# Eight low-part subtractions of the weight split, in four panels of the sparse attention, moved from VectorE to GpSimd

## The chip, the cores and the metric

The kernel runs on one core of a Trainium2 chip. The metric is the device time of one execution in microseconds. The core's engines are named as the profile names them: PE (TensorE, matmuls), PEld (its weight loads), DVE (VectorE), ACT (ScalarE), POOL (GpSimd) and SP (SyncE, which here issues most DMAs).

## The reference, cut to what matters

Two layers follow each other, each a token mixer, a layer norm, a squared-ReLU MLP and a layer norm. Layer 0 mixes tokens by a sparse attention: an indexer scores all earlier keys of a query, the best 128 are kept, and softmax attention runs over them. 512 tokens, model width 1024, all in 32-bit floats.

```python
def dsa_mixer(x, cos, sin, w_in, w_o):
    top_k = min(IDX_TOPK_MAX, L // 4)                 # 128
    proj = x @ w_in                                   # 512 x 1024 @ 1024 x 2120
    q, k, v, iq, ik, iw = jnp.split(proj, A_SPLITS, axis=-1)
    q, k, iq, ik = (partial_rotary(t, cos, sin) for t in (q, k, iq, ik))
...
    s = einsum('bqhd,bsd->bqhs', iq_b, ik) * IDX_DIM ** -0.5
    score = einsum('bqh,bqhs->bqs', iw_b, relu(s))    # causal keys only
    _, sel = lax.top_k(score, top_k)
    logits = einsum('bqgrd,bqkgd->bqgrk', q_b, k_sel) * A_HEAD_DIM ** -0.5
    p = softmax(logits)
    o = einsum('bqgrk,bqkgd->bqgrd', p, v_sel)
...
    return out @ w_o

for i in range(DEPTH):
    mix = dsa_mixer(h, ...) if i % 2 == 0 else gla_mixer(h, ...)
    h = layer_norm(DN_ALPHA * h + mix, ...)
    h = layer_norm(DN_ALPHA * h + squared_relu_mlp(h, ...), ...)
```

## The kernel before, in words

Every product of activations and weights is made of three matmuls on numbers rounded to the fast 32-bit format: high part by high part, high by low, low by high (`mm3`, lines 183 to 188). A weight matrix comes in panels, most of them 512 columns wide. A panel is loaded in four units of 256 rows by 512 columns (128 partitions by 1024 elements). For each unit SP issues one DMA into a `raw` tile (4 buffers), ACT rounds it into `w_hi` (line 130, 6 buffers), and DVE subtracts, `w_lo = raw - w_hi` (line 131, 6 buffers). `split` does the last two, `_load` loops over the two halves `ci` of a panel's rows and over `u`, the two units of each half. Below, "unit (p,n)" is the n-th of the four units of panel p, counted from 0: n is 2 ci + u, so u = 1 means n = 1 or 3.

`next_panel` loads one panel ahead: when the matmuls of panel p begin in the program, the instructions that load panel p+1 have just been written. The panels of the attention are 0 and 1 (indexer projections), 2 (keys and values), 3 and 4 (the two halves of the queries), 5 and 6 (output projection). The framework's scheduler then sets the order of the instructions on each engine, by its own estimates of when operands are ready; the engines work through these orders strictly one after the other and wait for each other by semaphores. The printed code is therefore not the order on an engine.

What stands around the loads in the attention, all of it on DVE as well:
- for each token tile of a projection `rotated` (lines 539 to 553) makes `rot_c`, `rot_s` and `nat`, and `stack_q` or `stack_k` form a high and a low part (`hl` in line 560, `dup` in line 578), which PE transposes (lines 567, 587) one tile later;
- `index_scores` (lines 609 to 622): PE makes `qk` for each of eight indexer heads (lines 613, 614; two buffers), ACT applies relu into `r` (line 616; two buffers), and DVE adds it to the scores `sc` (lines 618, 620);
- `top_k` (lines 655 to 665): for each of the query blocks 1 to 3, sixteen rounds of MAX8 (line 660) and MATCH_REPLACE8 (line 661) on the scores; the block widths are 256, 384 and 512 keys. A result of MAX8 is named `m_` and a number, in rising order; `sc_216`, `sc_217` and `sc_218` are the scores of blocks 1, 2 and 3;
- `logits` (lines 670 to 692): PE makes `qk`, DVE adds the mask and takes the maximum (line 685), ACT the exponential.

GpSimd is used elsewhere: in the MLP (`_load_forms`, lines 152 to 160, four subtractions of 128x1024 for every `down` panel but the last; `combine`), in the second layer's mixer, and for DMAs of layer norm parameters (lines 312, 313).

Of the kernel before, what the change touches and what calls it, by code (L numbers as in the profile page):

```python
# [14 lines left out]
F32 = mybir.dt.float32  # L15
# [8 lines left out]
P = 128  # L24
# [35 lines left out]
WARM_UP = (4, 6)  # L60
STACKED = 2
LAG = 3

_CF = {}

# [29 lines left out]
class Trunk:  # L95
# [26 lines left out]
            n += m  # L122
        return raw[:, :, :n]

    def split(self, src):

        n = src.shape[2]
        hi = self.w_p.tile([P, 2, 512], F32R, name="w_hi")[:, :, :n]
        lo = self.w_p.tile([P, 2, 512], F32R, name="w_lo")[:, :, :n]
        self.nc.scalar.copy(hi, src)  # L130
        self.nc.vector.tensor_sub(lo, src, hi.bitcast(F32))  # L131
        return hi, lo

    def _load(self, i):
        panel = self.panels[i]
        if isinstance(panel, tuple):
            return self._load_forms(*panel)
        units = {}
        for ci, (w, r0, nk, cols) in enumerate(panel):
            for u in range(nk // 2):  # L140
                hi, lo = self.split(self.fetch(w, r0 + 2 * u * P, cols))
                for j in range(2):
                    units[(ci, 2 * u + j)] = (hi[:, j, :], lo[:, j, :])
        return units
# [448 lines left out]
    def attention(self, x, xs):  # L593

        nc, tc = self.nc, self.tc
        with tc.tile_pool(name="att", bufs=1) as ap:
# [143 lines left out]
            def values_t(i, kb):  # L740

                b, g = steps[i]
                if kb == 0:
                    live["o"] = self.mm.tile([P, 512], F32, name="ps")
                ps = live["o"]
                ph, pl = (a.rearrange("p j q -> p (j q)") for a in live.pop((i, kb)))
                vs = live["vs"][:, kb * A_KV + g]
                vs = vs.rearrange("p two d -> p (two d)")
                nc.tensor.matmul(ps, vs, ph, start=kb == 0, stop=False)
                nc.tensor.matmul(ps, vs, pl, start=False, stop=kb == b)  # L750
                for f in live.pop("back", []):
                    f()
                if kb == b:
                    oT = ptp.tile([P, 4, P], F32, name="pT")
                    nc.scalar.copy(oT, ps.rearrange("p (j q) -> p j q", j=4))

                    def back():
                        po = self.po.tile([P, 512], F32, name="po").rearrange("p (j d) -> p j d", d=P)
                        for j in range(4):
                            nc.tensor.transpose(po[:, j, :], oT[:, j, :], self.ident)  # L760
                        on, rc = normalizer(b, g, live[i][2])
                        nc.scalar.copy(on, po[:, :, 64:128])
                        nc.vector.tensor_add(on, on, po[:, :, 0:64])
                        nc.vector.tensor_tensor(on, on, rc, op=OP.mult)
                        if g == A_KV - 1:
                            self.to_xt(live["on"], b)

                    live["back"] = [back]

            def blocks():  # L770
# [4 lines left out]
                for i, (b, g) in enumerate(steps):  # L775
                    if (b, g) == (STACKED, 0):
                        split_v()
                    for x in range(4):
                        if i + 1 < len(steps):
                            logits(i + 1, x)  # L780
                        if x <= b:
                            turn(i, x)
                            if b >= STACKED:
                                turned.append((i, x))
                        if len(turned) > LAG:
                            values_t(*turned.pop(0))
# [365 lines left out]
```

## Time and profile before

| | us |
|---|---|
| time, median of 3 executions (lowest to highest) | 1173.49 (1171.34 to 1174.58) |
| the profiled execution's own time | 1171.8 |
| its span, from the first to the last instruction | 1170.0 |
| PE busy in the span | 1147.4 |
| DVE busy | 901.1 |
| ACT busy | 559.3 |
| POOL busy | 213.8 |

The profile is of one execution. The busy times are of the whole span; an engine that is full in one stage and half idle in another shows a middling share. Matmuls are pipelined, so a PE that is shown busy may still have waited: its waits stand in the view of waits. The granted TensorE clock is shown as a share of full speed; over the span its mean is 0.996.

### The profile page before, as it was taken

Reading aid. Unit: us, or ns where it says so; the run is one execution under the profiler, and the core shown is the slowest. Engines: PE = TensorE matmul, PEld = TensorE weight load, DVE = VectorE, ACT = ScalarE, POOL = GpSimd, SP = SyncE. Lnnn points to the kernel's source line nnn. Section 1 sums busy time; section 2 is a strip of 40 time slices with the busy share of each in tenths; the row PEclk is TensorE's granted clock in tenths of the full one; section 3 lists DMA queues with packets and bytes.
Section 4 is the critical chain, followed back from the end, with each engine's and each line's share of the span. In section 5 each row is a group of like instructions: output and inputs, shape, how many; then the busy total and the mean of one; then the engine's idle time right before and its main releaser. Section 6 shows DMA issues by size and latency. Waiting matters only on the chain. (4 is left out here: it accounts for less than half of the span.)

```text
span 1170.0 us, 15763 instructions
## 1 busy us (share of the span) xinstructions
PE 1147.4 (98%) x5847; PEld 963.3 (82%) x5847; DVE 901.1 (77%) x1659; ACT 559.3 (48%) x953; POOL 213.8 (18%) x148
## 2 busy tenths in 40 slices
PE   8999999999999999999899999999999999999997
PEld 6877888888888888888788998778988888888875
DVE  6799997687876786687875477885787866886787
ACT  6665786543444353345356444443354533444342
POOL 0000000002223203222302254110032032223221
PEclk9999999999999999999999999999999999999999
DMA  5422130421431441243341231224214422431421
GB/s 199 142 73 73 36 109 1 144 73 37 144 99 46 143 141 64 84 144 94 91 133 49 61 104 41 73 75 142 73 54 127 140 64 85 144 103 44 142 72 73
DMA packets 57477, 109.36 MB, mean 93 GB/s; under 512 B 4708, under 2 KB 10088, under 8 KB 57400
## 3 DMA queue, kind: packets, MB, share of 16 engines
q1 hardware_dynamic: 56008, 103.44, 27.8%
q0 software_dynamic: 1392, 4.92, 1.4%
q8 instruction: 46, 0.75, 0.3%
q14 instruction: 31, 0.25, 0.1%
HBM read 106.24 MB, written 2.10 MB: 93 GB/s over the span
## 5 line engine op out<-in xcount | busy, mean ns | idle before, releaser
L131 DVE TENSOR_TENSOR w_lo<-raw,w_hi 128x1024 fp32r<-128x1024 f32 (+4 forms) x220 | 289.1, 1333 | 30.1 <-ACT w_hi L130 27.7
L130 ACT CAST w_hi<-raw 128x1024 fp32r<-128x1024 f32 (+4 forms) x220 | 223.6, 1024 | 117.7 <-PE ps L188 46.0
L186 PE MATMUL ps<-XT,w_hi 128*128 128x512 f32 (+1 forms) x640 | 236.0, 369 | 0.0
L187 PE MATMUL ps<-XT,w_hi 128*128 128x512 f32 (+1 forms) x640 | 235.5, 368 | 0.0
L188 PE MATMUL ps<-XT,w_lo 128*128 128x512 f32 (+1 forms) x640 | 235.5, 368 | 0.0
L186 PE MATMUL ps<-w_hi,XT 128*128 128x512 f32 (+5 forms) x440 | 164.3, 374 | 2.0 <-ACT XT L230 1.6
L187 PE MATMUL ps<-w_lo,XT 128*128 128x512 f32 (+5 forms) x440 | 161.7, 368 | 0.4 <-DVE w_lo L131 0.4
L188 PE MATMUL ps<-w_hi,XT 128*128 128x512 f32 (+5 forms) x440 | 161.2, 367 | 0.3 <-DVE XT L231 0.2
L186 PEld LDWEIGHTS ps<-XT,w_hi 128*128 128x128 f32 x640 | 120.7, 189 | 20.3 <-issue 0.2
L187 PEld LDWEIGHTS ps<-XT,w_hi 128*128 128x128 f32 x640 | 120.7, 189 | 20.2 <-issue 0.4
L188 PEld LDWEIGHTS ps<-XT,w_lo 128*128 128x128 f32 x640 | 120.6, 189 | 20.1 <-issue 0.2
L152 POOL TENSOR_TENSOR raw<-raw 128x1024 f32<-128x1024 f32 x14 | 34.2, 2441 | 385.3 <-DVE w_lo L131 385.3
L186 PE MATMUL ps<-w_hi,form 128*128 128x512 f32 x260 | 102.2, 393 | 0.7 <-DVE big L405 0.7
L187 PE MATMUL ps<-w_lo,form 128*128 128x512 f32 x260 | 101.4, 390 | 0.0
L188 PE MATMUL ps<-w_hi,form 128*128 128x512 f32 x260 | 101.4, 390 | 0.0
L186 PEld LDWEIGHTS ps<-w_hi,XT 128*128 128x128 f32 x440 | 83.3, 189 | 13.5 <-ACT XT L230 2.3
L188 PEld LDWEIGHTS ps<-w_hi,XT 128*128 128x128 f32 x440 | 83.4, 190 | 11.5 <-DVE XT L231 0.4
L187 PEld LDWEIGHTS ps<-w_lo,XT 128*128 128x128 f32 x440 | 83.4, 190 | 10.6 <-DVE w_lo L131 0.6
L131 DVE TENSOR_TENSOR w_lo<-t,w_hi 128x1024 fp32r<-128x1024 f32 x14 | 30.2, 2160 | 72.8 <-ACT w_hi L130 72.8
L357 DVE TENSOR_TENSOR h<-h 128x512 f32<-128x512 f32 (+1 forms) x72 | 43.7, 624 | 45.3 <-ACT h L356 45.3
L356 ACT ACTIVATE h<-ps 128x512 f32<-128x512 f32 (+1 forms) x72 | 38.6, 545 | 63.1 <-PE ps L188 56.1
L130 ACT CAST w_hi<-t 128x1024 fp32r<-128x1024 f32 x14 | 14.7, 1051 | 105.3 <-POOL t L154 105.3
(243 smaller groups left out, 2006.0 us busy)
## 6 DMA issues: line engine op xcount, KB each, us to landing
raw<-in_mlp_w_up_dram SPq DMA_DIRECT2D x64, 512.0 KB, 4.2
raw<-in_mlp_w_down_dram SPq DMA_DIRECT2D x64, 512.0 KB, 4.3
raw<-in_b_w_in_dram SPq DMA_DIRECT2D x16, 512.0 KB, 4.3
raw<-in_a_w_in_dram SPq DMA_DIRECT2D x12, 512.0 KB, 4.2
big<-in_x_dram SPq DMA_DIRECT2D x8, 512.0 KB, 4.1
raw<-in_a_w_o_dram SPq DMA_DIRECT2D x8, 512.0 KB, 4.6
raw<-in_b_w_o_dram SPq DMA_DIRECT2D x8, 512.0 KB, 4.9
raw<-in_b_w_in_dram SPq DMA_DIRECT2D x8, 346.0 KB, 3.7
```

What stands on the lines that cost most here:

```text
L130: self.nc.scalar.copy(hi, src)
L131: self.nc.vector.tensor_sub(lo, src, hi.bitcast(F32))
L152: sub(t1, b12, b11)
L186: mmul(out, lhs[0], rhs[0], start=first, stop=False, skip_group_check=more)
L187: mmul(out, lhs[0], rhs[1], start=False, stop=False, skip_group_check=more)
L188: mmul(out, lhs[1], rhs[0], start=False, stop=last, skip_group_check=more)
L356: nc.scalar.activation(h, ps[:, :step], AF.Relu)
L357: nc.vector.tensor_mul(h, h, h)
```

## The change

Units with u = 1 of the panels 2 to 5 get their low part on GpSimd; all other low parts stay on DVE. That is two units of four in four panels: eight instructions.

```diff
+POOL_PANELS = range(2, 6)
...
-    def split(self, src):
+    def split(self, src, pool=False):
...
         self.nc.scalar.copy(hi, src)
-        self.nc.vector.tensor_sub(lo, src, hi.bitcast(F32))
+        (self.nc.gpsimd if pool else self.nc.vector).tensor_sub(lo, src, hi.bitcast(F32))
...
-                hi, lo = self.split(self.fetch(w, r0 + 2 * u * P, cols))
+                hi, lo = self.split(self.fetch(w, r0 + 2 * u * P, cols), i in POOL_PANELS and u == 1)
```

The first added line moves the lines behind it by one: what is L131 before is L132 in the changed kernel. The scheduler makes new orders for all engines. Three places of them follow.

On POOL, from the start of the program, before (the DMAs are those of the layer norm parameters, the subtraction behind them the first of the MLP):

```order
L312 DMA lngb<-in_ln_mix_g_dram 128x1024
L313 DMA lngb<-in_ln_mix_b_dram 128x1024
L312 DMA lngb<-in_ln_mlp_g_dram 128x1024
L313 DMA lngb<-in_ln_mlp_b_dram 128x1024
L152 ISA
L152 TENSOR_TENSOR raw<-raw 128x1024
```

and in the changed kernel:

```order
L132 ISA
L132 TENSOR_TENSOR w_lo<-raw,w_hi 128x1024 x8
L313 DMA lngb<-in_ln_mix_g_dram 128x1024
L314 DMA lngb<-in_ln_mix_b_dram 128x1024
L313 DMA lngb<-in_ln_mlp_g_dram 128x1024
L314 DMA lngb<-in_ln_mlp_b_dram 128x1024
```

The eight subtractions stand ahead of everything that POOL did before.

On DVE, where the second half of panel 2 and the first half of panel 3 are split, with buffer numbers, before (`w_lo_486` is unit (2,2), `w_lo_492` (2,3), `w_lo_674` (3,0), `w_lo_680` (3,1)):

```order
L131 TENSOR_TENSOR w_lo_486<-raw_483,w_hi_485 128x1024
L131 TENSOR_TENSOR w_lo_492<-raw_489,w_hi_491 128x1024
L560 TENSOR_TENSOR hl_575<-nat_568,hl_575 128x5x64
L131 TENSOR_TENSOR w_lo_674<-raw_671,w_hi_673 128x1024
L550 TENSOR_TENSOR rot_c_614<-ps_578,cos_93 128x80
L551 TENSOR_TENSOR rot_s_615<-ps_578,sin_92 128x80
L131 TENSOR_TENSOR w_lo_680<-raw_677,w_hi_679 128x1024
L552 TENSOR_TENSOR nat_612<-rot_c_614,rot_s_615 128x5x16
L618 TENSOR_SCALAR sc1_216<-r_625,iw_230 128x256
```

and in the changed kernel:

```order
L132 TENSOR_TENSOR w_lo_486<-raw_483,w_hi_485 128x1024
L561 TENSOR_TENSOR hl_575<-nat_568,hl_575 128x5x64
L132 TENSOR_TENSOR w_lo_674<-raw_671,w_hi_673 128x1024
L551 TENSOR_TENSOR rot_c_614<-ps_578,cos_93 128x80
L552 TENSOR_TENSOR rot_s_615<-ps_578,sin_92 128x80
L553 TENSOR_TENSOR nat_612<-rot_c_614,rot_s_615 128x5x16
L619 TENSOR_SCALAR sc1_216<-r_625,iw_230 128x256
L561 TENSOR_TENSOR hl_619<-nat_612,hl_619 128x5x64
```

Two subtractions are gone from DVE's order; the rest stands as before. The two that are gone run on POOL while DVE is between these rows.

On DVE, where the third token tile of the second half of the queries (panel 4) gets its low part, `hl`, before:

```order
L661 MATCH_REPLACE sc_218<-m_1832,sc_218 128x512
L550 TENSOR_TENSOR rot_c<-ps,cos 128x128
L551 TENSOR_TENSOR rot_s<-ps,sin 128x128
L660 MAX m_1835<-sc_218 128x8
L552 TENSOR_TENSOR nat<-rot_c,rot_s 128x8x16
L661 MATCH_REPLACE sc_218<-m_1835,sc_218 128x512
L660 MAX m_1886<-sc_218 128x8
L131 TENSOR_TENSOR w_lo<-raw,w_hi 128x1024
L560 TENSOR_TENSOR hl<-nat,hl 128x8x64
L131 TENSOR_TENSOR w_lo<-raw,w_hi 128x1024
L661 MATCH_REPLACE sc_218<-m_1886,sc_218 128x512
```

and in the changed kernel:

```order
L661 MAX m_1892<-sc_218 128x8
L662 MATCH_REPLACE sc_218<-m_1892,sc_218 128x512
L551 TENSOR_TENSOR rot_c<-ps,cos 128x128
L552 TENSOR_TENSOR rot_s<-ps,sin 128x128
L661 MAX m_1895<-sc_218 128x8
L553 TENSOR_TENSOR nat<-rot_c,rot_s 128x8x16
L662 MATCH_REPLACE sc_218<-m_1895,sc_218 128x512
L664 TENSOR_SCALAR sc_218<-sc_218 128x512
L132 TENSOR_TENSOR w_lo<-raw,w_hi 128x1024
L561 TENSOR_TENSOR hl<-nat,hl 128x8x64
L132 TENSOR_TENSOR w_lo<-raw,w_hi 128x1024
```

All rounds of the selection for block 3 now stand ahead of this `hl` (the last is `m_1895`, and line 664 closes it), where before the rounds of `m_1886` (its MATCH_REPLACE), `m_1889`, `m_1892` and `m_1895` came behind it. On PE the same transposes stand at the same counts of projection matmuls, but for two groups that moved ahead by 5 and by 3 matmuls, and the eight heads of the first index scores, which stand closer together.

## Rows read from the trace of the kernel before

**Rows 1.** The page, part 1: busy us, share of the span and instructions of each engine.

```profile
PE 1147.4 (98%) x5847; PEld 963.3 (82%) x5847; DVE 901.1 (77%) x1659; ACT 559.3 (48%) x953; POOL 213.8 (18%) x148
```

**Rows 2.** Windows: stretch, length, busy us of PE, PEld, DVE, ACT, POOL; clock, DMA.

```profile
30.00:40.00 10.00, 10.00 (x69) 9.98 (x68) 4.08 (x11) 4.83 (x12) 0.00 (x0) 0.94 0.52 182
40.00:137.00 97.00, 95.32 (x513) 77.35 (x512) 94.33 (x272) 61.15 (x123) 0.00 (x0) 1.00 0.21 66
137.00:180.00 43.00, 42.40 (x303) 37.09 (x302) 39.63 (x123) 38.10 (x94) 0.00 (x0) 1.00 0.30 99
180.00:270.00 90.00, 89.63 (x530) 77.06 (x529) 62.67 (x143) 45.54 (x95) 2.27 (x4) 1.00 0.22 71
```

**Rows 3.** Waits of PE and PEld from 40 to 180: total us, times, longest.

```profile
PE qk L683 <- DVE mx L685: 0.8, 3, 0.4
...
PEld qk L613 <- ACT r L616: 2.7, 10, 0.5
PEld qk L683 <- DVE mx L685: 2.6, 6, 0.8
```

**Rows 4.** Waits of PE and PEld from 137 to 180.

```profile
PE tps L698 <- DVE XT L231: 0.3, 1, 0.3
...
PEld tps L698 <- DVE XT L231: 0.6, 1, 0.6
...
PEld tps L698 <- DVE pT L707: 0.3, 1, 0.3
```

**Rows 5.** DVE groups by form, 40 to 270: count, busy us, mean ns, idle before.

```profile
L131 DVE TENSOR_TENSOR w_lo<-raw,w_hi 128x1024 fp32r<-128x1024 f32 x24 | 28.8, 1218 | 1.7 <-ACT w_hi L130 1.6
...
L660 DVE MAX8 m<-sc 128x8 f32<-128x512 f32 x16 | 11.0, 685 | 0.1
L661 DVE MATCH_REPLACE8 sc<-m,sc 128x512 f32<-128x512 f32 x16 | 10.8, 676 | 0.0
...
L661 DVE MATCH_VALUE_LOAD sc<-m,sc 128x8 f32 x48 | 4.1, 85 | 0.6
...
L663 DVE TENSOR_SCALAR sc<-sc 128x512 f32<-128x512 f32 x1 | 0.4, 420 | 0.0
```

**Rows 6.** Line 131, the whole span: ns lowest/median/highest, first and last start.

```profile
L131 DVE TENSOR_TENSOR w_lo<-raw,w_hi x220: 700/1210/3477, 8.1 to 1136.1; 128x1024 fp32r<-128x1024 f32 x100, 128x692 fp32r<-128x692 f32 x4, 128x528 fp32r<-128x528 f32 x2, 128x640 fp32r<-128x640 f32 x2
...
L131 DVE TENSOR_TENSOR w_lo<-t,w_hi x14: 1208/2315/2325, 288.4 to 1107.9; 128x1024 fp32r<-128x1024 f32 x14
```

**Rows 7.** Timeline of POOL and of DVE in the first MLP: start, us, line.

```profile
276.59 2.72 POOL L152 TENSOR_TENSOR raw<-raw 128x1024 f32<-128x1024 f32 x1 [56.33 <-DVE w_lo L131]
279.39 2.74 POOL L154 TENSOR_TENSOR t<-raw 128x1024 f32<-128x1024 f32 x1
...
276.37 0.68 DVE L374 TENSOR_TENSOR big<-h 128x512 f32<-128x512 f32 x1
277.08 2.77 DVE L375 TENSOR_TENSOR big<-big,h 128x512 f32<-128x512 f32 x1
```

**Rows 8.** Timeline: POOL with DVE quiet (318.10), POOL beside a PSUM-reading DVE (559.35).

```profile
318.10 2.39 POOL L152 TENSOR_TENSOR raw<-raw 128x1024 f32<-128x1024 f32 x1 [20.52 <-DVE w_lo L131]
...
559.35 2.55 POOL L444 TENSOR_TENSOR big<-big 128x512 f32<-128x512 f32 x2
...
559.35 0.67 DVE L445 TENSOR_TENSOR big<-big,qk 128x512 f32<-128x512 f32 x1
```

**Rows 9.** Timeline of ACT and DVE at the second place of the change.

```profile
42.15 1.06 ACT L130 CAST w_hi<-raw 128x1024 fp32r<-128x1024 f32 x1
...
42.94 0.23 DVE L550 TENSOR_TENSOR rot_c<-ps,cos 128x80 f32<-128x80 f32 x1
...
44.38 0.23 DVE L552 TENSOR_TENSOR nat<-rot_c,rot_s 128x80 f32<-128x80 f32 x1
```

**Rows 10.** Timeline of DVE and PE at the third place of the change.

```profile
136.10 0.68 DVE L560 TENSOR_TENSOR hl<-nat,hl 128x512 fp32r<-128x512 f32 x1
...
137.76 0.80 PE L567 MATMUL tps<-ident_r,hl 128*128 128x128 f32 x8
```

## The prediction, made before the changed kernel ran

> **What bounds the kernel now.** First the page's busy times [rows 1]: PE is busy for 1147.4 of 1170.0 us, so nothing that frees another engine can help except where PE waits for that engine. Then the attention by windows [rows 2]. From 40 to 137 us DVE is busy for 94.33 of 97.00 us, from 137 to 180 for 39.63 of 43.00; before 40 it is less than half busy, after 180 at 70%. POOL does nothing up to 180. The eight subtractions that move lie in this stretch, the first at 30 us, the others from 40 to 137. So DVE is nearly full where the change takes work from it. The third view is what PE waits for there [rows 3]: of 140 us only 0.8 and 2.6 us are put to the maxima that DVE takes of the logits, and 2.7 us to ACT's relu in the index scores, which in its turn waits for DVE to free `r`. The reader is to see a gap between the two: DVE is full, but PE hardly waits for it, because DVE has a backlog, the rounds of the selection, that the scheduler has fitted in between what PE needs soon. The sum is therefore made along DVE, up to a place where PE takes something from it.
>
> **The change, part by part.** The place is the `hl` of the third token tile of panel 4 (third place of the change). DVE makes it at 136.10, it ends at 136.78, and PE begins its transposes at 137.76 [rows 10]: 1.0 us of slack.
>
> What leaves DVE ahead of it: seven subtractions of 1.218 us [rows 5], 8.5 us; the eighth, unit (5,3), lies behind. One of the seven, (2,1), lies at 30 us, where DVE is idle for 6 of 10 us [rows 2], and gives nothing. That leaves 6 x 1.218 = 7.3 us.
>
> What comes ahead of it: in the order on DVE all rounds for block 3 now precede it. Four MATCH_REPLACE8 of 0.676 with their value loads of 0.085, three MAX8 of 0.685 and line 664's 0.420 [rows 5]: 2.7 + 0.3 + 2.1 + 0.4 = 5.5 us. These are not new work: they stood behind it and are missing there. So DVE reaches this `hl` only 7.3 - 5.5 = 1.8 us earlier, if nothing else happens.
>
> What else happens: POOL needs 2.39 us for a subtraction of this size with DVE quiet [rows 8], and while it runs, DVE doesn't get on with some of its own. In the MLP a DVE subtraction of a size that takes 0.68 us just before, issued at 277.08, during a POOL subtraction that ends at 279.31, takes 2.77 us, and POOL's next one, issued at 279.39, then takes 2.74 [rows 7]. Over the whole span the longest `w_lo` is 3.477 us against a median of 1.210, and those that read `t`, issued when POOL is half through, take 2.315 [rows 6]. They read both operands from SBUF. An operation of the same size as the 0.68 us ones that reads one operand from PSUM takes 0.67 us beside POOL [rows 8]. So a DVE operation with two SBUF operands stands until POOL is done, and since DVE works in order, all that is behind it stands too. When both want to begin, the one that waited goes first: POOL's op at 276.59 was issued during a DVE op that ran to 277.05, and got in ahead of the one at 277.08.
>
> The price of one subtraction on POOL lies between 0 (DVE has 2.4 us of other work at hand) and 3.477 - 1.210 = 2.27 us (the next operation is of that kind); 1.1 us (2.315 - 1.210) is the middle case. For the six this is 0 to 13.6 us. I take it from the new order. (2,3) starts as DVE finishes (2,2), and the next on DVE is `hl`, two SBUF operands: 2.3 us. (3,1) becomes ready when its `w_hi` ends at 43.2 [rows 9] and, with `hl` held, DVE is in (3,0) then; behind it come `rot_c` and `rot_s`, which read PSUM, 0.23 us each, and then `nat`, which doesn't: 2.39 - 0.46 = 1.9 us. There the index scores of block 1 wait for it: lines 618 and 620 stand behind `nat` on DVE, ACT's `r` has two buffers, PE's `qk` two, and PE's order now has the eight heads closer together; so PE should stop here first, near 44 to 48 us. For (3,3), (4,1), (4,3) and (5,1) the order has one or two rounds of the selection before the next `nat`, `hl` or `w_lo`: the middle case, 4 x 1.1 = 4.4 us. Together 8.6 us.
>
> Line 663, a tensor_scalar on one SBUF operand, stands behind (3,3)'s start too; I count it as not held. The Trainium skill, SBUF — State Buffer, Who interferes with whom, says that tensor_scalar can run in a mode that uses the port which VectorE shares with GpSimd, and then stands until GpSimd is done. By that the hold of (3,3) would rise from the middle case to the whole 2.27 us, and the sum by 1.2 us, to +5.8; by the middle case it is +4.6. No run shown here has line 663 beside POOL.
>
> So DVE reaches the `hl` 8.6 - 1.8 = 6.8 us late, and with 1.0 us of slack PE is 5.8 us late. Behind it DVE has 5.5 us less to do and one subtraction less. PE can use that only as far as it waits for DVE there: 0.3, 0.6 and 0.3 us [rows 4], 1.2 us. From 180 on DVE has room, and PE's order is work from end to end. The sum: +5.8 - 1.2 = +4.6 us. The profiled execution took 1171.8 us, so 1176.4; the median of the three runs stands 1.7 us above that one, and the forecast against it is 1173.5 + 4.6 = 1178 us, slower by 0.4%.
>
> Edits costed at nothing. A low part is ready some 1.2 us later, or more where POOL waits; its unit is the second of a half panel, and PE reads it half a token tile after the first, or, for panels 4 and 5, long after. If that cover is gone, PE waits for POOL by as much. The `raw` buffer comes free later by the same time, and SP's next load with it; four buffers stand between, and in this stretch the DMA engines are busy for 0.21 [rows 2]. The layer norm parameters are queued on POOL behind the eight; POOL did nothing with them up to 180 us [rows 2].
>
> **The rivals.** *Faster.* DVE's holds fall on operations that don't mind, under 0.3 us each: 6 x 0.3 = 1.8 us, where the term of the order is used up, decides. Then PE gains what it waits for DVE: at most 0.8 + 2.6 + 2.7 = 6.1 us [rows 3], but 1.8 us up to the `hl` and 1.2 us behind it are what the order allows, and 1 us of its waits in the logits on top: -4 us, 1169.5. For it speaks that MAX8 and MATCH_REPLACE8, the bulk of DVE's work here, read one SBUF operand; against it the `hl` and `nat` that follow at once at the second place.
>
> *No change.* The holds average 0.5 to 1 us, 3 to 6 us in all; less 1.8 us and 1.0 us of slack PE is 0 to 3 us late and makes good 1.2 us: 1173 to 1176, say 1175. For it speaks that each of the eight was placed where POOL is free from the start, and that part of a hold can fall into the 2.7 us that DVE is idle from 40 to 137 [rows 2].
>
> *Much slower.* MAX8 and MATCH_REPLACE8 are held as well. No row shows either of them beside POOL. Then each of the six costs DVE its whole 2.39 us: 14.3 - 1.8 - 1.0 - 1.2 = +10 us, 1184. The nearest rows, the operation that reads PSUM and writes SBUF beside POOL undisturbed [rows 8] and the held ones with two SBUF operands [rows 7], put it nearer to not held, as one stream from SBUF is what they share with the first.
> The Trainium skill, SBUF — State Buffer, Who interferes with whom, says that a VectorE instruction with at most one SBUF input, outside the modes that use both ports, does not contend with GpSimd, and no run here shows that for MAX8. By that rule this rival falls, and the sum stays as it is.
>
> **How the numbers follow.** Slower by the sum, 1175.5 to 1181: 0.43. No change: 0.30. Faster: 0.20. Much slower: 0.07. About 0.3%, 3.5 us, is what a measurement of this kernel can tell from no change. The first case reaches a little below that bound and the second a little above it, so: faster by over 0.3% 0.20, within 0.30, slower 0.50. The range leaves out the outer half of the faster case and of the much slower one, and what is beyond them: 1169.5 to 1185. It holds both signs; the likeliest case alone has 1175.5 to 1181.
>
> **What would show it.** Eight subtractions of about 2.4 to 3.5 us on POOL from 30 to 140 us. `hl` and `nat` of DVE near 40 to 47 us that take 1.9 to 2.8 us in place of 0.48 and 0.23, and PE waiting for ACT's `r` there for 2 us more than now: if they keep their lengths, the price of a hold is wrong. MAX8 and MATCH_REPLACE8 at their 0.68 us: if they grow, it is the last rival. The `hl` of the third place some 6 us later than 136.1, and the stretch behind it with fewer waits of PE for DVE. If instead this `hl` comes no later than 136, the change gains; if it comes late and the end of the attention does not, PE had more room to make it good than the waits show. The MLPs and the second layer should take what they took.

## The result: 1.2% slower, three times the forecast

The changed kernel takes 1186.91 us (median of 4 executions, 1182.62 to 1190.46), the kernel before 1172.45 beside it: a ratio of 1.0123, 95% interval 1.0105 to 1.0140, or 14.4 us. The forecast was 1178 us, +4.6, with a range up to 1185. The direction was right, and so was the mechanism of the holds; what PE makes of them, and with it the size, was not. The profiled execution took 1186.95 us, its span is 1185.2.

Part 1 of the page of the changed kernel, which answers to [rows 1]:

```profile
PE 1154.5 (97%) x5847; PEld 970.2 (82%) x5847; DVE 907.0 (77%) x1651; ACT 560.0 (47%) x953; POOL 235.5 (20%) x156
```

DVE has eight instructions less, 1651 for 1659, and yet 5.9 us more of busy time: what was taken from it came back as length of others. Two of the windows of [rows 2]; the columns are stretch, length, busy us of PE, PEld, DVE, ACT, POOL, the granted clock, DMA:

```profile
40.00:137.00 97.00, 88.58 (x454) 72.64 (x453) 91.85 (x248) 55.04 (x110) 15.74 (x6) 0.93 0.22 66
137.00:180.00 43.00, 41.35 (x290) 36.95 (x289) 34.61 (x104) 33.08 (x74) 2.77 (x1) 1.00 0.23 74
```

Two things are new from 40 to 137 us. PE is busy for 88.58 us where it was busy for 95.32, and the granted clock is 0.93 where it was 1.00. The second comes from short stretches at half clock, 1.2 GHz for 2.4. This execution has five before the end of the program, the first ahead of POOL's first subtraction, the last far behind the change:

```profile
10.10:16.90 6.80, 6.14 (x26) 5.40 (x27) 2.98 (x8) 3.66 (x8) 0.00 (x0) 0.50 0.88 315
47.60:51.00 3.40, 2.85 (x10) 2.56 (x11) 2.34 (x5) 1.85 (x6) 0.00 (x0) 0.50 0.78 245
85.20:92.00 6.80, 6.28 (x20) 5.11 (x21) 5.82 (x15) 1.95 (x4) 0.00 (x0) 0.50 0.37 123
129.50:133.00 3.50, 3.50 (x20) 3.38 (x20) 3.30 (x16) 2.31 (x7) 0.00 (x0) 0.51 0.00 0
590.30:593.80 3.50, 3.50 (x10) 2.72 (x9) 2.73 (x5) 1.60 (x5) 0.00 (x0) 0.51 0.01 2
```

The first does not go with the change: of the thirteen profiles of this document seven have a stretch of 3.4 or 6.8 us between 10 and 34 us, that of the kernel before among them (27.8 to 31.2), and six have none.

The waits of PE from 40 to 200 us, which answer to [rows 3] (total us, times, longest):

```profile
PEld qk L684 <- DVE mx L686: 5.2, 9, 2.0
PEld qk L614 <- ACT r L617: 5.0, 9, 3.2
...
PE qk L684 <- DVE mx L686: 3.1, 4, 1.7
...
PE qk L614 <- ACT r L617: 2.8, 1, 2.8
...
PE tps L588 <- ACT dup L578: 2.6, 1, 2.6
...
PE tps L568 <- DVE hl L561: 1.0, 1, 1.0
```

PE now stops. The longest stops are one each in the index scores (line 614, from 45.4 us), at the transposes of the last keys (line 588, from 83.1), of a query's `hl` (line 568, from 116.5) and in the logits (line 684, from 125.3 and 152.1). Of the four later half-clock stretches two begin within such a stop, 2.2 and 2.1 us after its start, and one 2.5 us after the end of one; the last, at 590.3, begins 1.2 us after the end of a stop of 3.17 us at the start of the second layer, which the kernel before has too.

Where DVE's lateness comes from is seen in the timeline of POOL and DVE (start, us, engine, line). At the second place of the change:

```profile
40.97 2.50 POOL L132 TENSOR_TENSOR w_lo<-raw,w_hi 128x1024 fp32r<-128x1024 f32 x1 [6.01 <-ACT w_hi L131]
41.29 2.53 DVE L561 TENSOR_TENSOR hl<-nat,hl 128x320 fp32r<-128x320 f32 x1
43.74 1.21 DVE L132 TENSOR_TENSOR w_lo<-raw,w_hi 128x1024 fp32r<-128x1024 f32 x1
44.14 3.03 POOL L132 TENSOR_TENSOR w_lo<-raw,w_hi 128x1024 fp32r<-128x1024 f32 x1 [0.66 <-ACT w_hi L131]
44.88 0.23 DVE L551 TENSOR_TENSOR rot_c<-ps,cos 128x80 f32<-128x80 f32 x1
45.03 0.23 DVE L552 TENSOR_TENSOR rot_s<-ps,sin 128x80 f32<-128x80 f32 x1
45.29 1.98 DVE L553 TENSOR_TENSOR nat<-rot_c,rot_s 128x80 f32<-128x80 f32 x1
```

`hl` stands from its issue to 43.8, just after POOL is done at 43.47; `rot_c` and `rot_s`, which read PSUM, keep their 0.23 us beside POOL, and `nat`, 0.23 before [rows 9], takes 1.98. The third stop of DVE, beside (3,3):

```profile
78.42 2.44 POOL L132 TENSOR_TENSOR w_lo<-raw,w_hi 128x1024 fp32r<-128x1024 f32 x1 [31.25 <-ACT w_hi L131]
...
78.58 0.41 DVE L662 MATCH_REPLACE8 sc<-m,sc 128x256 f32<-128x256 f32 x1
78.90 0.55 DVE L661 MAX8 m<-sc 128x8 f32<-128x384 f32 x1
79.37 1.63 DVE L664 TENSOR_SCALAR sc<-sc 128x256 f32<-128x256 f32 x1
```

MATCH_REPLACE8 and MAX8 run beside POOL at their own length, and the tensor_scalar of line 664, 0.27 us in the kernel before, stands until POOL is done. The first and the last of the eight subtractions hold something too, a `dup` that takes 0.22 us elsewhere, where DVE has idle time, and a `w_lo` of 1.22 us:

```profile
32.57 2.40 POOL L132 TENSOR_TENSOR w_lo<-raw,w_hi 128x1024 fp32r<-128x1024 f32 x1 [32.12 <-ACT w_hi L131]
32.85 2.20 DVE L579 TENSOR_TENSOR dup<-nat,dup 128x64 fp32r<-128x64 f32 x1 [0.42 <-ACT dup L578]
...
148.42 2.77 POOL L132 TENSOR_TENSOR w_lo<-raw,w_hi 128x1024 fp32r<-128x1024 f32 x1 [33.22 <-ACT w_hi L131]
149.64 2.64 DVE L132 TENSOR_TENSOR w_lo<-raw,w_hi 128x1024 fp32r<-128x1024 f32 x1 [0.70 <-ACT w_hi L131]
```

### The profile page after: what moved, and what is told of

Its sections match the earlier page's. It is cut to its first block, busy times and chain, and to the rows that moved or that the text cites. A ratio compares the mean times of both kernels' runs of the same rounds, so it can differ in the third digit from the quotient of the medians.

```text
span 1185.2 us, 15769 instructions
## 1 busy us (share of the span) xinstructions
PE 1154.5 (97%) x5847; PEld 970.2 (82%) x5847; DVE 907.0 (77%) x1651; ACT 560.0 (47%) x953; POOL 235.5 (20%) x156
## 3 DMA queue, kind: packets, MB, share of 16 engines
q1 hardware_dynamic: 56008, 103.44, 27.8%
## 5 line engine op out<-in xcount | busy, mean ns | idle before, releaser
L132 DVE TENSOR_TENSOR w_lo<-raw,w_hi 128x1024 fp32r<-128x1024 f32 (+4 forms) x212 | 282.3, 1347 | 31.1 <-ACT w_hi L131 28.6
L131 ACT CAST w_hi<-raw 128x1024 fp32r<-128x1024 f32 (+4 forms) x220 | 223.7, 1024 | 118.7 <-PE ps L189 47.6
L132 DVE TENSOR_TENSOR w_lo<-t,w_hi 128x1024 fp32r<-128x1024 f32 x14 | 30.2, 2161 | 72.8 <-ACT w_hi L131 72.8
L131 ACT CAST w_hi<-t 128x1024 fp32r<-128x1024 f32 x14 | 14.7, 1051 | 105.3 <-POOL t L155 105.3
```

Of the source, the lines that this page charges most:

```text
L132: (self.nc.gpsimd if pool else self.nc.vector).tensor_sub(lo, src, hi.bitcast(F32))
```

## The experiments

All ran 6 to 12 times beside the kernel before, which took 1171.67, 1172.17 and 1171.79 us in the three groups.

**The orders without the work.** The edit (low parts left out):

```diff
-        lo = self.w_p.tile([P, 2, 512], F32R, name="w_lo")[:, :, :n]
         self.nc.scalar.copy(hi, src)
-        (self.nc.gpsimd if pool else self.nc.vector).tensor_sub(lo, src, hi.bitcast(F32))
-        return hi, lo
+        if not pool: self.lo = self.w_p.tile([P, 2, 512], F32R, name="w_lo")[:, :, :n]
+        if not pool: self.nc.vector.tensor_sub(self.lo, src, hi.bitcast(F32))
+        return hi, self.lo
```

> The eight low parts are not formed at all (each of these units reads the low tile of the unit before it), so this run leaves part of the computation out. The orders on PE, on DVE, on ACT and on SP are, row for row, those of the changed kernel; only POOL's eight subtractions are gone. Theory A (POOL's subtractions hold DVE, DVE is late, PE stops): nothing is held, DVE is relieved of eight subtractions, and the time is not above that of before: 1166 to 1173 us. Rival B (the changed orders themselves, with the rounds of the selection ahead of what PE needs, make PE wait): the time stays at 1178 to 1187 us. Rival C (the low parts come too late for PE from the slower engine): as A here, so this run tells only B apart; A and C are told apart by the run with POOL's work added to the kernel before.

Measured: 1175.58 us, ratio 1.0036 (1.0024 to 1.0049). Between the two. The holds are gone, and with them 10.2 us of the 14.4; but the orders alone, with eight subtractions less on DVE, do not gain, they lose 4.2 us (0.0036 x 1172). PE has one long stop left in the attention, in the first logits, and a half-clock stretch of 13.6 us behind it (the timeline of PE, then a window):

```profile
112.12 0.44 PE L187 MATMUL ps<-w_hi,XT 128*128 128x512 f32 x1
113.89 0.33 PE L684 MATMUL qk<-kT,big 128*128 128x128 f32 x1 [1.32 <-DVE mx L686]
```

```profile
115.60:129.20 13.60, 13.52 (x66) 12.98 (x64) 9.65 (x44) 8.10 (x21) 0.00 (x0) 0.50 0.00 1
```

In the kernel before the longest of these waits is 0.4 us [rows 3]. So 1.3 us of a stop and a longer stretch behind it: this is what made the clock the next question.

**The work without the orders.** The edit: DVE keeps all low parts, and POOL makes the same subtraction once more, into the raw tile, when DVE is done with it.

```diff
-        (self.nc.gpsimd if pool else self.nc.vector).tensor_sub(lo, src, hi.bitcast(F32))
+        self.nc.vector.tensor_sub(lo, src, hi.bitcast(F32))
+        if pool: self.nc.gpsimd.tensor_sub(src, src, hi.bitcast(F32))
```

> The kernel before, with all low parts on DVE and in the same orders on PE, DVE, ACT and SP, and eight subtractions of the same size on POOL beside it, whose results nobody reads. Theory A (holds): DVE's operations with two operands in SBUF stand until POOL is done, 1 to 2 us each, with no work taken from DVE in return; PE stops near 44 to 50 us and again behind 80 us, and TensorE's clock falls after these stops as it did in the changed kernel: 1180 to 1192 us. Rival B (order) and rival C (a low part late for PE): no change, 1171 to 1176 us, since the orders are those of before and no matmul reads what POOL makes.

Measured: 1181.51 us, ratio 1.0091 (1.0075 to 1.0107): theory A, and B and C fall as the main cause. The held operation is now the next of DVE's own `w_lo`, and behind it a scalar_tensor_tensor with two SBUF operands, 0.48 us when alone:

```profile
42.86 2.58 POOL L132 TENSOR_TENSOR raw<-raw,w_hi 128x1024 f32<-128x1024 f32 x1 [8.78 <-DVE w_lo L131]
48.09 2.49 POOL L132 TENSOR_TENSOR raw<-raw,w_hi 128x1024 f32<-128x1024 f32 x1 [2.65 <-issue]
...
43.10 3.43 DVE L131 TENSOR_TENSOR w_lo<-raw,w_hi 128x1024 fp32r<-128x1024 f32 x1
...
48.50 2.36 DVE L621 SCALAR_TENSOR_TENSOR sc<-r,iw,sc 128x256 f32<-128x256 f32 x1
```

**What POOL does while DVE waits.** The same kernel with zeros written, or one operand copied, in place of the subtraction:

```diff
-        if pool: self.nc.gpsimd.tensor_sub(src, src, hi.bitcast(F32))
+        if pool: self.nc.gpsimd.memset(src, 0.0)
```

> As the run with eight subtractions added on POOL to the kernel before, but POOL writes zeros into the same tiles in place of subtracting; the orders on all other engines are those of before. Theory A in its narrow form (POOL's reading of SBUF is what holds DVE): nothing is held, 1170 to 1174 us. Rival (any work of POOL on these tiles holds DVE, or the later freeing of the raw tile delays the loads): slower by 3 us or more, 1175 to 1182 us.

Measured: 1172.73 us, ratio 1.0005 (0.9994 to 1.0015). Theory A.

```diff
+        if pool: self.nc.gpsimd.tensor_copy(src, hi.bitcast(F32))
```

> As the run with eight subtractions added on POOL to the kernel before, but POOL copies one operand in place of subtracting two. Theory A: a POOL operation that reads SBUF once holds DVE's operations with two SBUF operands as well, for as long as it runs, so 1174 to 1181 us, by the length that the copy turns out to have. Rival (only POOL operations with two operands in SBUF hold DVE): 1170 to 1174 us, and hl and nat beside the copy at 0.48 and 0.23 us.

Measured: 1174.19 us, ratio 1.0019 (1.0008 to 1.0030): at the low end of theory A, since the copy takes only 1.09 us (median) where the subtraction takes 2.4. DVE beside POOL, first with the zeros, then with the copy:

```profile
39.74 0.96 POOL L132 MEMSET raw<- 128x1024 f32 x1 [7.66 <-DVE w_lo L131]
42.77 0.95 POOL L132 MEMSET raw<- 128x1024 f32 x1 [2.07 <-issue]
...
40.00 1.22 DVE L131 TENSOR_TENSOR w_lo<-raw,w_hi 128x1024 fp32r<-128x1024 f32 x1
...
42.73 1.14 DVE L619 TENSOR_SCALAR sc<-r,iw 128x256 f32<-128x256 f32 x1
```

```profile
41.89 1.25 POOL L132 COPY raw<-w_hi 128x1024 f32<-128x1024 f32 x1 [7.57 <-DVE w_lo L131]
45.76 1.20 POOL L132 COPY raw<-w_hi 128x1024 f32<-128x1024 f32 x1 [2.62 <-issue]
...
42.14 2.06 DVE L131 TENSOR_TENSOR w_lo<-raw,w_hi 128x1024 fp32r<-128x1024 f32 x1
...
46.17 1.05 DVE L621 SCALAR_TENSOR_TENSOR sc<-r,iw,sc 128x256 f32<-128x256 f32 x1
```

A `w_lo` beside a POOL that only writes takes its 1.22 us; beside one that reads it takes 2.06 us and stands until POOL is done. These kernels also free the raw tile later, as the change does, so that edit costs nothing, as the prediction had it.

**Shorter pieces on POOL.** Each of the eight as two of 128x512, the orders of the other engines unchanged:

```diff
+        for c in ([slice(0, 1), slice(1, 2)] if pool else [slice(0, 2)]):
+            (self.nc.gpsimd if pool else self.nc.vector).tensor_sub(lo[:, c], src[:, c], hi[:, c].bitcast(F32))
```

> The changed kernel with each of the eight subtractions on POOL made as two of 128x512; the orders on PE, DVE, ACT and SP are unchanged. Theory A (DVE's operation stands until POOL's running one is done, and the one that waited goes first): a hold ends with the half that runs, so no hold is longer than about 1.3 us, where it was 1.4 to 2.1, and the stops of PE behind them are shorter: 1177 to 1183 us. Rival: POOL keeps the two halves together, or DVE is held twice: 1184 to 1190 us as before the cut.

Measured: 1184.99 us, ratio 1.0108 (1.0085 to 1.0131). A miss: a little less than 1.0123, and its interval overlaps. The holds did get shorter:

```profile
38.76 1.42 DVE L561 TENSOR_TENSOR hl<-nat,hl 128x320 fp32r<-128x320 f32 x1
40.10 2.31 DVE L132 TENSOR_TENSOR w_lo<-raw,w_hi 128x1024 fp32r<-128x1024 f32 x1
...
42.74 0.90 DVE L553 TENSOR_TENSOR nat<-rot_c,rot_s 128x80 f32<-128x80 f32 x1
43.57 1.36 DVE L619 TENSOR_SCALAR sc<-r,iw 128x256 f32<-128x256 f32 x1
```

`hl` takes 1.42 for 2.53 and `nat` 0.90 for 1.98, but each half holds something, so `w_lo` and line 619 are held as well. PE's stops are shorter, 1.7, 1.5 and 1.7 us for 2.8, 2.6 and 1.7, and behind the first two follows half clock again. This profile is of the shortest of the six executions, 1179.86 us, with a mean clock of 0.993; the other five took 1184.57 to 1189.21 at 0.984 to 0.988. So what the shorter holds gave was for the most part lost again in time at half clock; behind which stops, no profile shows.

**Panel by panel.** The range of panels alone is changed.

```diff
-POOL_PANELS = range(2, 6)
+POOL_PANELS = range(2, 3)
```

> Only the two units of panel 2 go to POOL, (2,1) and (2,3). Theory A: the first falls in idle time of DVE; the second holds an hl for 2 us, and PE stops once for about 2 us in the first index scores, near 44 to 48 us; a stretch at half clock behind it would add 1.7 us: 1174 to 1177 us. Rival B: by its own order, no forecast below +1 us. If the losses of the changed kernel don't come from one place each, but only all together, this run stands within 1 us of before.

Measured: 1178.93 us, ratio 1.0051 (1.0033 to 1.0068).

> Only the two units of panel 3 go to POOL. If the losses of the changed kernel add up over places, the full-speed part (span times mean granted clock) of the runs with panel 2, panel 3 and panels 4 and 5 alone should add to that of the whole: 5.2 us in all, of which panel 2 gave -0.5 and panels 4 and 5 gave 3.8, so about 2 us for this one, and some 3 to 6 us more at half clock: 1175 to 1181 us. If each new order has stops of its own that have nothing to do with where POOL works, this run can lie anywhere from 1172 to 1182 us, and its stops are not at places where a DVE operation was held.

Measured: 1177.60 us, ratio 1.0044 (1.0028 to 1.0059).

> Only the four units of panels 4 and 5 go to POOL. In the changed kernel PE lost about 4.6 us from 110 to 160 us, partly at half clock. Theory A: holds of about 1 us each on nat and w_lo, less what DVE is relieved of: 1173 to 1178 us. If the lateness that costs time is all from panels 2 and 3, as places before the third token tile of panel 4 would have it, this run is not slower than before: 1169 to 1173 us.

Measured: 1180.91 us, ratio 1.0092 (1.0071 to 1.0113). All three slower, and they don't add up: 6.0, 5.2 and 10.8 us (the ratios on 1172) make 22 us for 14.4 of the whole. Each has an order of its own, and a stop or two of its own. Those of panel 3 alone are one behind a hold (line 614, 1.9 us), a short one at line 588 (0.7 us) and one, in the first logits, where POOL has been done for 39 us (line 684, 1.3 us, the stop of the run without the work). So the split by panels tells no more than that no single panel carries the loss.

**The clock.** Matmuls that nobody reads were put into PE's order in front of the instructions at which it stops, with every other order as it was:

```diff
+FILL = ((614, 3, 12), (588, 32, 11), (568, 48, 4), (684, 2, 7), (684, 22, 4), (229, 96, 14))
...
+    for line, nth, n in fill:
+        at = row.index([i for i in mms if i.debug.lineno == line][nth])
+        for _ in range(n):
+            nc.tensor.matmul(po[:, :], one, xt[:, 0, 0, :], start=True, stop=True)
+            row.insert(at, last.pop())
```

> The changed kernel, its orders unchanged, with matmuls that nobody reads put into PE's order just before six instructions at which it stops: 12, 11, 4, 7, 4 and 14 of 128x512, 0.21 us each, a little less than each stop is long, so that PE works through most of the stop and goes on at the same moment. All else, POOL's work and the holds of DVE included, stays. Theory A with the clock (a stop of PE is what the half clock follows, and the half clock is two thirds of the loss): the full-speed part (span times mean granted clock) grows by at most 1 us, the part lost to the clock falls from 14.2 us to the 5 us of the kernel before, and the time to 1175 to 1179 us. Rival (the clock falls for another reason, the stops being incidental): 1184 to 1192 us as without the filling.

Measured: 1180.65 us, ratio 1.0078 (1.0063 to 1.0092). The half clock behind the stops is gone, and with it 5.3 us; the rest is not. The windows of this kernel and its first filled stop:

```profile
40.00:137.00 97.00, 95.40 (x509) 76.92 (x509) 93.38 (x257) 57.73 (x116) 16.83 (x6) 1.00 0.22 66
...
580.00:600.00 20.00, 19.76 (x96) 15.99 (x95) 16.96 (x51) 9.91 (x23) 0.00 (x0) 1.00 0.11 33
```

```profile
45.36 0.39 PE L188 MATMUL ps<-w_lo,XT 128*128 128x512 f32 x1
45.59 2.88 PE L1141 MATMUL po<-XT,ident_r 128*128 128x512 f32 x12
48.59 0.38 PE L614 MATMUL qk<-ikT,iqT 128*128 128x256 f32 x1
```

From 40 to 137 us the clock is 1.00 in place of 0.93. Line 614 starts at 48.59 where it started at 48.15, and 0.39 of these 0.44 us stood at 41 us already (table below): the filling took the place of the stop and did not lengthen it. The expectation put two thirds of the loss on the clock, by taking span times clock as the part at full speed. That was wrong. The three stretches in the attention of the changed kernel, 13.7 us, cost 2.9 us (table below), less than half their length, presumably because PE would have waited for DVE in part of them anyway. The one at the end of the program is in the kernel before as well. The one at the start does cost time, up to 3.2 us, but it comes in some executions and not in others, and these runs do not tie it to the change.

Two more runs with filled stops, the kernel before with one of the six places, and the run without the work with two:

> The kernel before with 14 such matmuls in front of the transposes at the start of the second layer, where PE stops for 3.15 us in every profile so far, and nothing else. If half clock follows that stop in a part of the executions, it now follows in none: 0 to 1.7 us less than before, 1170 to 1172 us. If the matmuls cost more than they hide: 1172 to 1175 us.

Measured: 1171.64 us, ratio 0.9989 (0.9978 to 1.0000): 0 to 2.6 us less.

> The run without the eight low parts (left out, so part of the computation is missing), with 6 matmuls in front of its one new stop, in the first logits, and 14 at the start of the second layer. It shows what the change could bring at most, if POOL's work held nobody and cost nothing. By the full-speed part of that run, 1164.7 us against 1165.5 before, and 4 to 5 us at half clock: 1169 to 1171 us, at most 0.2% below before. If the relief of DVE were worth what the rival of the prediction gave it, 4 us, it would be 1168 us or less.

Measured: 1171.05 us, ratio 0.9996 (0.9987 to 1.0005). This is the floor of the idea: with the low parts for nothing, no hold and no half clock behind a stop, it stands where the kernel before stands. With these orders no other way of making the eight low parts can be expected to beat the kernel before by more than that, so none was tried; other orders were not tried either.

## Why the prediction was right in direction and wrong in size

The runs split the 14.4 us into parts: once by the medians (ratios times 1172, with about a 95% interval), once by the profiled executions, from 41 us to the end of the attention.

| step | runs compared | us, medians | us, profiles | forecast |
|---|---|---|---|---|
| relief of DVE and new orders, no work on POOL, stops filled | 0.9996 against 0.9989 | +0.8 ± 1.7 | +0.9 | -1.8, -1.0 (slack) and -1.2 (recovered) |
| POOL's subtractions hold DVE, stops filled | 1.0078 against 0.9996 | +9.6 ± 2.0 | +9.1 | +8.6 |
| half clock behind the stops | 1.0123 against 1.0078 | +5.3 ± 2.7 | +2.9 | none |

The medians sum to 15.7; the kernel before with its stop filled stands 1.3 us below the one that changed here, which leaves 14.4. The profiles are compared at instructions that all five kernels have at the same count of PE's matmuls (start in us; in the kernel before the lines are 567 and 698):

| profiled execution | PE, `tps` of line 568 | DVE, `hl` of the third place | PE, last `tps` of line 699 in the attention |
|---|---|---|---|
| before | 40.48 | 136.10 | 214.78 |
| before, one stop filled | 38.71 | 134.33 | 212.96 |
| changed, without the work, two stops filled | 38.55 | 134.59 | 213.69 |
| changed, six stops filled | 41.73 | 145.74 | 225.94 |
| changed | 41.34 | 148.25 | 228.39 |

Two pairs of these rows, of the run with six filled stops and of the run without the work:

```profile
41.73 0.54 PE L568 MATMUL tps<-ident_r,hl 128*128 128x128 f32 x5
225.94 0.66 PE L699 MATMUL tps<-cft,pr 128*128 128x128 f32 x4
```

```profile
38.55 0.54 PE L568 MATMUL tps<-ident_r,hl 128*128 128x128 f32 x5
213.69 0.65 PE L699 MATMUL tps<-cft,pr 128*128 128x128 f32 x4
```

From the first to the last it is 184.2 us in the one and 175.1 in the other, 9.1 us for the holds. The first column differs by up to 3.2 us, and it is the profiles with a half-clock stretch at the start that stand behind. Behind the attention the changed kernel loses another 0.9 us against the one with filled stops, as PE's last matmuls show (1176.57 and 1173.20 us), at the start of the second layer. So the half clock behind the new stops cost about 3 us in these profiles and that behind the old one about 1; the rest of the 5.3 is inside its interval. Part of it can be the stretch at the start, since four of the six executions with filled stops show a mean clock of 0.998 or more and can hardly have it.

**The price of the holds: right.** The six operations and their lengthening in the trace: `hl` 0.48 to 2.53, `nat` 0.23 to 1.98, line 664 0.27 to 1.63, `nat` 0.21 to 1.64, `w_lo` 1.22 to 2.05, `nat` 0.28 to 1.44. That is 2.05 + 1.75 + 1.36 + 1.43 + 0.83 + 1.16 = 8.6 us, the sum that was forecast, and nearly each by its own value (2.3, 1.9 and four times 1.1). That POOL has to read SBUF to hold an operation with two SBUF operands is shown by the runs with zeros (`w_lo` 1.22 us) and with a copy (2.06). Two more operations were held, outside the sum: `dup` from 0.22 to 2.20 by (2,1), which cost PE nothing, as forecast, and `w_lo` from 1.22 to 2.64 by (5,3), which was not priced at all and is followed by a stop of PE.

**Line 664 not held: wrong** (663 in the prediction's numbering). It stood 1.36 us longer. The Trainium skill, SBUF — State Buffer, Who interferes with whom, names tensor_scalar among the operations that can contend with GpSimd, and the trace agrees with it. The 2.27 us that it could have cost did not come about, because POOL's subtraction had begun 0.95 us earlier; so the middle case, 1.1, was close for (3,3) for a reason other than the one given.

**The last rival's mechanism: refuted.** MAX8 at 0.55 and 0.69 us and MATCH_REPLACE8 at 0.41 and 0.67 us beside POOL keep their lengths. The Trainium skill, SBUF — State Buffer, Who interferes with whom, says so of operations with one SBUF input outside the modes that use both ports. The time went beyond that rival's 1184 all the same, by another way.

**From DVE's lateness to PE's: the step that failed.** "DVE reaches the `hl` 8.6 - 1.8 = 6.8 us late, and with 1.0 us of slack PE is 5.8 us late", less 1.2 us recovered. None of the three subtracted terms, 1.8, 1.0 and 1.2 us, was seen. By the second table, counted from its first column, the new orders and the relief of DVE bring the `hl` of the third place 0.4 us later, not 1.8 earlier; the holds bring it 8.0 us later and the half clock 2.9. That makes 11.3 us where 6.8 were forecast (148.25 in place of 136.10 is 12.2, of which 0.9 stood at 41 us already). The sum was made at one place, as if relief gained anywhere ahead of it could pay for a hold anywhere ahead of it. But PE takes something from DVE every few us, and it stopped on the way: 2.8 us at 45.4, 2.6 at 83.1, 1.0 at 116.5, 1.7 at 125.3, 0.9 at 152.1, 9.0 us together. Four of the five stand behind a hold, the last of them behind that of (5,3). The one at 125.3, in the first logits, is for the most part one of the new orders, since the run without the work has it too, with 1.3 us. By the matmul ahead of the `hl` of the third place the holds had made PE itself 8.0 us late, so there was no lateness of DVE alone for the 1.0 us of slack to take up. What DVE saves behind a stop doesn't bring that stop back: the 9.1 us of the holds at the end of the attention are 9.3 at PE's last matmuls (1173.20 against 1160.74, less the 3.2 of the first column). And the run without the work shows the relief together with the new orders, the holds and the stops away: 0.9 us lost in the profiles, 0.8 ± 1.7 by the medians, none gained. That DVE had a backlog was seen; that PE therefore gains nothing when it shrinks, and loses when something it needs soon is held, was only half drawn from it.

**The clock: a term that was missing.** The prediction took every us of a stop as one us. [Rows 2] showed the clock at 1.00 from 40 to 270 in a kernel that nearly never stopped there, and nothing was asked about a kernel that stops. Here stops of 1.3 to 2.8 us were followed by 3.4 to 13.6 us at 1.2 GHz; filling them took 2.9 us off the attention of the changed kernel and 4.6 off that of the run without the work (from line 568 to line 699 179.7 us, and 175.1 filled). The Trainium skill, TensorE: Matmul & The Clock Gate, HAM oscillation — how this bites in real kernels, tells of a loop whose bursts each start at half clock after a wait for a DMA. The traces here show the same behind single stops, shorter than the waits told of there, though not behind every one.

**The rest.** The eight subtractions took 2.4 to 3.0 us on POOL from 32.6 to 148.4, as forecast. From 40 to 200 us no wait of PE is for a `w_lo`. The start of the second layer changed after all, by a half-clock stretch at 590 us behind a stop of 3.17 us that was there before. Of the ten profiles in which that stop is not filled seven have such a stretch, two of them with the orders of the kernel before and work added on POOL; the kernel before's own has none.

## What to carry to other kernels

Work moved from VectorE to GpSimd is not taken away if both sides read SBUF: count each VectorE operation with two SBUF operands, and each tensor_scalar, that comes next in order as standing until GpSimd is done. Where PE is full and takes small results from a full VectorE, price each hold at the first thing PE needs behind it and don't set relief elsewhere against it; then leave room for half clock behind the stops, here 4 to 5 us on 9 us of stops, though not every stop brings it. A run that leaves the work to be moved out altogether shows first what there is to gain: here nothing. And look at where half clock lies before comparing two profiled executions: a stretch at the start of the program alone set some of these apart by 3 us.

## What was not expected of the hardware

- Filling a stop of PE with idle matmuls keeps the clock at full speed: 40 to 137 us at 1.00 for 0.93, 1180.65 us for 1186.91. Not every stop is followed by half clock: the 3.15 us at 572 us of the kernel before was not in its profile, nor were four stops of 1.65 to 1.85 us in four of the other runs. And four profiles, that of the kernel before among them, fall to half clock near 27 us where PE had no stop over 0.42 us since 15 us, and others with the same stops do not. So the length of a stop did not settle it here.
- A POOL operation that only writes SBUF left `w_lo` alone (1.22 us) but seems to have held a tensor_scalar: line 619 took 1.14 us beside it, 0.34 in the changed kernel. This is one instance.
- On POOL 128x1024 elements take 0.95 us to set, 1.09 to copy and 2.4 to subtract.
